# Other widths for four weight groups, and other places for steps in a hand-written order: a change to a two-layer hybrid encoder trunk

## The chip, the core and the metric

The kernel runs on one core of a Trainium2 chip. The metric is the device time of one execution in microseconds (us). Five engines work side by side on a core, each through its own instructions in order: TensorE (PE in the profile, PEld its weight loads), VectorE (DVE), ScalarE (ACT), GpSimd (POOL) and SyncE (SP). Here SP only issues DMAs, and POOL issues DMAs and clears a few tiles.

## The reference

`x` is 256 rows of 2048 columns, `mem` 256 rows of the same width. Two layers follow each other. A layer multiplies `x` by one wide input matrix and cuts the product into eleven parts:

```python
h = x @ w_in
a_q, a_k, a_v, a_z, b_q, b_k, b_v, b_z, b_lr, m_q, m_z = jnp.split(h, cuts, axis=-1)
y_a = chunk_band_attention(a_q, a_k, a_v, rel_table)     # 8 heads of 128
o_b = gla_chunk_recurrence(b_q, b_k, b_v, log_g)         # 4 heads, chunks of 64
y_m = memory_attention(m_q, mk, mv)                      # 4 heads, mk, mv = mem @ w_mem_kv
y = jnp.concatenate([y_a * silu(a_z), y_b * silu(b_z), y_m * silu(m_z)], axis=-1)
x = layer_norm(DEEPNORM_ALPHA * x + y @ w_out, ln_g, ln_b)
```

Group A is softmax attention with a relative bias, group B gated linear attention (GLA) whose gates come from a product of rank 16 (`b_lr`), group M softmax attention into the memory. `y_b` is `o_b` after an RMS norm.

## The kernel before, in words

**Groups and pieces.** Every large product is done in groups. A group is a stripe of weight columns, up to 512 wide, against all 2048 rows of the weight: eight pieces of two k-slices each (`as_group`, L274). For a piece SP loads the fp32 weights into `raw`, ACT writes a rounded copy `wh`, and DVE subtracts to get the rest, `wl` (`piece`, L136, and `parts`, L122). PE then does three products for each k-slice and each of two row blocks: high x with high weight, low x with high weight, high x with low weight (`as_products`, L266). So a piece is twelve matmuls and a group 96. `raw`, `wh` and `wl` have four buffers each, so at most four converted pieces, and four raw ones behind them, can lie ready ahead of PE. The sums of a group stand in a pair of PSUM banks, of which there are two pairs (`psd`).

**Turned data.** Q, K, gates and softmax rows must be transposed for their next use. `turned` (L530) does that without PE: DVE transposes blocks of 32 by 32 into a scratch tile, POOL writes it to a DRAM tile `home`, and four more POOL DMAs read it back in the other order. The reader of the turned tile is either PE itself or a generator that copies it once more (`placed`, L521; `gated`, L509; `gla_turned`, L493; `norm_rows`, L692).

**The order.** PE and SP run in exactly the order in which the program issues instructions. DVE, ACT and POOL are put in order by a planner with its own estimates of times and with priorities; the work of `piece` has a high priority (`AHEAD`). Small work is written as Python generators, and a step of one is let in between two pieces of a group. `tick` (L52) does that: it moves a counter on, by 1 for a piece of 512 columns and by n / 512 for a narrower one (L285). First it runs the entries of `side` whose due time has come. Then it runs one step of one `active` generator that is due. A generator yields the number of ticks until its next step. `waiting` holds generators not yet begun; two may be active while GLA runs, three afterwards. `finish` (L76) ticks until given generators are done, without issuing pieces.

**A layer.** Memory values and keys; in layer 1 also the transposes of the normalised `x`, and `restored`. Then a group for GLA's q and k, then the values: 1552 columns (16 of `b_lr`, 512 of `b_v`, 1024 of `a_v`) in four groups of 388 (`values`, L850). Two of these stand ahead of the loop over `half` at L878, one in each round behind Q and K of four heads. GLA begins with the first round, and its steps lie between the pieces. `finish(laid)` at L883 waits until the turned Q and K of the round have been handed over; then its four heads join `waiting`. The memory queries follow the loop (L888), then the gate groups BZ, AZ0, AZ1 and MZ, each SiLU-ed, turned and multiplied by `gated` or `gla_gate` into the operands `yq` of the output product. The output groups take these operands in quarters: the dictionary `need` says at which piece which `gated` must be done (L908, L959). Each output group adds the residual `res` (L660) and collects statistics; the layer norm follows. In layer 0 `res` is loaded from `xn` by one DMA at L862, after the second value group. The last layer loads `ln_g` and `ln_b` as rows, converts them and writes them into four-row tiles (`norm_rows`); they are read in the last matmuls.

**Due times.** `staged` (L804) puts `placed` on `side` 5 ticks after the group that was turned (L809). `gated` is due 6 ticks after its group (L909). `gla_turned` waits 2 and then 6 ticks (L499). A head of group A (`a_head`) does its scores and softmax, waits 9 ticks for the turned probabilities, does the values' product, and ends 2 ticks later. A memory head (`m_head`) waits 7 (L599), converts, waits 2, multiplies, and ends 2 later.

Of the kernel before, what the change touches and what calls it, by code (L numbers as in the profile page):

```python
# [9 lines left out]
F32R = mybir.dt.float32r  # L10
# [8 lines left out]
P = 128  # L19
# [17 lines left out]
def hybrid_trunk_kernel(  # L37
# [84 lines left out]
    def parts(hi, lo, src):  # L122

        act.copy(hi, src)  # L124
        dve.tensor_tensor(lo, src, hi.bitcast(F32), op=ALU.subtract)  # L125
# [10 lines left out]
    def piece(src, n, kp=2, home=None):  # L136

        with tc.high_priority(AHEAD):
            raw = wp.tile([P, kp, n], F32, name=nm("raw"), tag="raw")
            if home is None:  # L140
                hi, lo = (wp.tile([P, kp, n], F32R, name=nm(w), tag=w) for w in ("wh", "wl"))
            else:
                hi, lo = home
            if isinstance(src, list):
                w = n // len(src)
                for i, part in enumerate(src):
                    sp.dma_start(raw[:, :, i * w:(i + 1) * w], part.rearrange("p (k n) -> p k n", k=kp))
            else:
                sp.dma_start(raw.rearrange("p k n -> p (k n)"), src)
            parts(hi, lo, raw)  # L150
        return hi, lo
# [122 lines left out]
    def as_group(src, xq, n, kp=2, first=None, need={}):  # L274

        acc = psd.tile([P, 2, 512], F32, name=nm("acc"), tag="acc")
        for pc in range(16 // kp):
            if first is not None and pc % 2 == 0:
                xq.append(load_quarter(first[pc // 2]))
            finish(need.get(pc, ()))  # L280
            w = piece(src[pc], n, kp)
            for kk in range(kp):
                for t in range(2):
                    as_products(acc[:, t, :n], t, xq, w, pc * kp + kk, kk)
            tick(n / 512)  # L285
        return acc
# [206 lines left out]
    def gla_turned(yraw, ng, y):  # L493

        yT = []
        for par in range(2):
            yT.append(hd.tile([P, 4, P], F32, name=nm("yT"), tag=("gq", "gk")[par]))
            turned(P, (yT[par], yraw[:, 2 * par:2 * par + 2].rearrange("p t d -> p (t d)")))
            yield 2 + 4 * par  # L499
        for par in range(2):  # L500
            for t in range(2):
                for b in range(2):
                    hi, lo = (x.rearrange("p k (t a j) -> p k t a j", t=2, j=32)[:, b * 2 + par, t] for x in y[:2])
                    src = yT[par].rearrange("p a (t b j) -> p t b a j", t=2, j=32)[:, t, b]
                    act.activation(hi, src, AF.Copy, scale=ng[:, 0:1])
                    dve.scalar_tensor_tensor(lo, src, ng[:, 0:1], hi.bitcast(F32), op0=ALU.mult, op1=ALU.subtract)
            yield 1
# [67 lines left out]
    def m_head(h, q, mk, mv, y, laid):  # L575

        while not all(g in done for g in laid):
            yield 1
        pb = bank()
        for t in range(2):  # L580
            o = pb[:, t * 256:(t + 1) * 256]
            qh, ql = (x[:, h, t * P:(t + 1) * P] for x in q)
            kh, kl = (x[:, h] for x in mk)
            mm(o, qh, kh, True, False)
            mm(o, ql, kh, False, False)
            mm(o, qh, kl, False, True)
        mx = small([P, 2], "mx", 4)
        zs = small([P, 2], "zs", 4)
        dve.tensor_reduce(mx, pb.rearrange("p (t m) -> p t m", t=2), AX.X, ALU.max, negate=True)
        dve.tensor_scalar(mx, mx, SCALE, None, op0=ALU.mult)  # L590
        s = scratch([P, 2, 256])
        for t in range(2):
            act.activation(s[:, t], pb[:, t * 256:(t + 1) * 256], AF.Exp, bias=mx[:, t:t + 1], scale=SCALE, accum_out=zs[:, t:t + 1])
        dve.reciprocal(zs, zs)
        for t in range(2):
            dve.tensor_scalar(s[:, t], s[:, t], zs[:, t:t + 1], None, op0=ALU.mult)
        pT = hd.tile([P, 4, 128], F32, name=nm("pT"), tag="qe" if h % 2 else "gb_")
        turned(128, (pT, s.rearrange("p t m -> p (t m)")))
        yield 7  # L599
        ph, pl = scratch([P, 2, 256], F32R), scratch([P, 2, 256], F32R)  # L600
        for t in range(2):
            parts(*(x.rearrange("p m (t a j) -> p t m a j", t=2, j=32)[:, t] for x in (ph, pl)),
                  pT.rearrange("p a (t m j) -> p t m a j", t=2, j=32)[:, t])
        yield 2
        po = bank()
        for m in range(2):
            vh, vl = (x[:, m, h * P:(h + 1) * P] for x in mv)
            mm(po[:, 0:256], vh, ph[:, m], m == 0, False)
            mm(po[:, 0:256], vl, ph[:, m], False, False)
            mm(po[:, 0:256], vh, pl[:, m], False, m == 1)  # L610
        act.copy(y, po[:, :256])
        yield 2
# [76 lines left out]
            pool.dma_start(raw[i * 16:i * 16 + 16], src[l].rearrange("(k p) -> k p", p=P))  # L689
        return raw, hd.tile([P, 32], F32, name=nm("gbT"), tag="pairs1")  # L690

    def norm_rows(l):  # L692

        rows = []
        for i in range(2):
            cs = slice(i * 1024, (i + 1) * 1024)
            raw, hi, lo, both = (hd.tile([P, 1024], F32R if j else F32, name=nm("gbrow"), tag="qk", bufs=4)
                                 for j in range(4))
            pool.dma_start(raw[0:1], ln_g[l:l + 1, cs])
            pool.dma_start(raw[1:2], ln_b[l:l + 1, cs])  # L700
            parts(hi[:2], lo[:2], raw[:2])
            pool.dma_start(both[0:2], hi[:2])
            pool.dma_start(both[2:4], lo[:2])
            rows.append(both)
        return rows

    def norm_last(accs, rest, stats, gb, rows, more):

# [91 lines left out]
    for l in range(L):  # L800
# [3 lines left out]
        def staged(g, x, raw, place):  # L804
            acc = as_group(halves(g), x, 512)
            raw = raw.rearrange("p (t a) n -> p t a n", t=2) if raw.shape[2] == P else raw.rearrange("p (t a) (b n) -> p t (a b) n", t=2, n=P)
            turned(P, *((raw[:, t], acc[:, t]) for t in range(2)))
            gen = placed(raw, place)
            side.append((gen, now[0] + 5))  # L809
            return [gen]  # L810

        mk = [per.tile([P, 4, T], F32R, name=nm("mk"), tag=f"mk{i}") for i in range(2)]
# [34 lines left out]

        asv = per.tile([P, 2, 1552], F32, name=nm("asv"), tag="asv")

        def values(i):  # L850
            acc = as_group(w388[l, i], xq, 388)
            act.copy(asv[:, :, i * 388:(i + 1) * 388], acc[:, :, :388])

        lr = hd.tile([P, 2, P], F32R, name=nm("lr"), tag="qe")
        pool.memset(lr.bitcast(F32), 0.0)
        values(0)
        for i in (0, 32):
            act.copy(lr[:, :, i:i + 16], asv[:, :, :16])
        dve.tensor_tensor(lr[:, :, 16:32], asv[:, :, :16], lr[:, :, :16].bitcast(F32), op=ALU.subtract)
        values(1)  # L860
        if l == 0:
            sp.dma_start(res, xn.rearrange("(t p) d -> p t d", p=P))  # L862
        bias = {}

        def load_bias(h):
# [9 lines left out]
        gens = [[gla(*gp, gq, gk, lr, asv, yraw[0])]]  # L875
        waiting.extend(gens[0])
        linear[:] = gens[0]
        for half in range(2):  # L878
            q, k = (hd.tile([P, 4, T], F32, name=nm("qk"), tag="qk", bufs=4) for _ in range(2))
            laid = staged(G_AQ0 if half == 0 else G_AQ1, xq, yraw[3], lambda src, at, q=q: act.copy(at(q), src))  # L880
            laid += staged(G_AK0 if half == 0 else G_AK1, xq, k, None)
            values(2 + half)
            finish(laid)  # L883
            kv = k.rearrange("p x y -> p (x y)").rearrange("p (ta g j) -> p g ta j", g=4, j=32)
            gens.append([a_head(half * 4 + h, load_bias, bias, q[:, h], kv[:, h], asv, yraw[1 + half][:, h]) for h in range(4)])
            waiting.extend(gens[-1])
        q = [hd.tile([P, 4, T], F32R, name=nm("mq"), tag="qk", bufs=4) for _ in range(2)]
        laid = staged(G_MQ, xq, yraw[3], lambda src, at: parts(at(q[0]), at(q[1]), src))  # L888
        gens.append([m_head(h, q, mk, mv, yraw[3][:, h], laid) for h in range(4)])
        waiting.extend(gens[-1])  # L890


# [7 lines left out]
        for i, g in ((1, G_AZ0), (2, G_AZ1), (3, G_MZ)):  # L900
            acc = as_group(halves(g), xq, 512)
            yq.append(operand())
            zT = hd.tile([P, 2, 4, P], F32, name=nm("zT"), tag="qk", bufs=4)
            sz = [scratch([P, 512]) for _ in range(2)]
            for t in range(2):
                act.activation(sz[t], acc[:, t], AF.Silu)  # L906
            turned(P, *((zT[:, t], sz[t]) for t in range(2)))
            need[i * 2] = [gated(zT, yraw[i], gens[i], yq[i])]  # L908
            side.extend((x, now[0] + 6) for x in need[i * 2])  # L909
        finish(gens[0])  # L910


# [5 lines left out]
            for dst, src in zip(gb[n], (ln_g, ln_b)):  # L918
                pool.dma_start(dst, src[l:l + 1, columns(n)].to_broadcast([P, 512]))

        rows = norm_rows(l) if last else None
        for n in range(WO_N):
            if last:
                gb.append((scratch([P, 512]), scratch([P, 512])))
# [139 lines left out]
```

## Time and profile before

| | us |
|---|---|
| three runs: lowest, median, highest | 906.75, 909.83, 910.12 |
| the profiled execution | 906.32 |
| its span, first to last instruction | 904.5 |
| granted TensorE clock, mean | 0.998 |
| DMA moved in the span | 211.34 MB, mean 234 GB/s |

The profile is of one execution. Its page gives the busy time of each engine, the span in 40 slices (a digit is the busy share in tenths), the chain of work that ended last, and the costliest groups of instructions. A group line reads: line, engine, operation, output tile `<-` input tiles, shape, count `|` busy us, mean ns of one `|` idle us of the engine just before them, and what ended the idle time. In timelines a row is start us, duration us, engine, line, operation, tiles, shape, count, and in brackets the idle time before it and its releaser. In the chain in order of time a row is start us, us, engine, tile, line and count. In the list of waits a row is: who waited `<-` for whom: us in total, times, longest. A row of stretches has the window, its length, the busy us (and count) of PE, PEld, DVE, ACT and POOL, the granted clock, the DMA share and GB/s. Matmuls are pipelined and their ends are modelled, so starts are safer than durations. L102 is the one line that issues all matmuls, L124 and L125 are the two operations of `parts`, so tiles tell the groups apart: `acc` is a group's PSUM tile, `bk` a single bank for small work, `wh` and `wl` the converted weights.

### The profile page before, as it was taken

The page shows a single profiled execution, that of the slowest core. Times are in us where ns is not written, and L with a number is a line of the kernel's source. Part 1 is how long each engine was busy: PE and PEld are TensorE (multiplying, and loading weights), DVE is VectorE, ACT ScalarE, POOL GpSimd, SP SyncE. Part 2 cuts the span into 40 slices and gives each one's busy share as a digit, 9 for nine tenths or more (in the row PEclk, how much of TensorE's full clock was granted, in tenths as well). Part 3 has the DMA queues.
Part 4 walks back from the last instruction along what each step waited for, and adds up shares of the span by engine and source line. Part 5 has one row for each costly group of instructions (what it writes and reads, how often), then busy time and mean ns, then how long its engine had stood idle before and what let it go on. Part 6 is the DMA issues. An engine that isn't in the chain of part 4 may idle for free.

```text
span 904.5 us, 13856 instructions
## 1 busy us (share of the span) xinstructions
PE 897.8 (99%) x4798; PEld 768.2 (85%) x4798; DVE 607.2 (67%) x878; ACT 477.2 (53%) x687; POOL 197.8 (22%) x369
## 2 busy tenths in 40 slices
PE   9999999999999999999999999999999999999997
PEld 8889988988988888888888898898898888888885
DVE  6765478766566676565587676777756586666766
ACT  6654465574545566433476445655744465655440
POOL 0002012116243553200000220221071434334000
PEclk9999999999999999999999999999999999999999
DMA  9977976858977998776675687658698879888652
GB/s 308 324 210 212 310 234 183 262 167 259 273 230 224 265 275 264 232 254 192 210 247 192 201 250 224 203 186 249 189 267 242 261 218 276 253 260 274 211 164 93
DMA packets 145974, 211.34 MB, mean 234 GB/s; under 512 B 15464, under 2 KB 117224, under 8 KB 145648
## 3 DMA queue, kind: packets, MB, share of 16 engines
q1 hardware_dynamic: 130544, 173.28, 61.5%
q0 software_dynamic: 15072, 36.79, 14.3%
q8 instruction: 37, 0.61, 0.3%
q10 hardware_dynamic: 288, 0.39, 0.1%
q14 instruction: 33, 0.27, 0.1%
HBM read 192.02 MB, written 18.35 MB: 233 GB/s over the span
## 4 chain that ended last, share of the span: by engine, by line
PE 99%; DMA 0%; DVE 0%; ACT 0%; issue 0%
PE acc L102 90%; PE bk L102 8%; PE bk L630 0%; DMA raw<-w 0%; PE bk L399 0%; ACT res L786 0%; DVE stats L771 0%; PE bk L346 0%; DVE res L770 0%; ACT wh L124 0%; DVE res L722 0%; DVE mvt L725 0%; PE bk L774 0%; ACT nparts L124 0%; DVE rs_u L733 0%
## 5 line engine op out<-in xcount | busy, mean ns | idle before, releaser
L102 PE MATMUL acc<-wh,x 128*128 128x512 f32 (+2 forms) x2452 | 736.9, 382 | 0.2 <-ACT wh L124 0.2
L102 PEld LDWEIGHTS acc<-wh,x 128*128 128x128 f32 x2452 | 453.7, 188 | 73.5 <-ACT wh L124 0.5
L125 DVE TENSOR_TENSOR wl<-raw,wh 128x1024 fp32r<-128x1024 f32 (+3 forms) x321 | 368.1, 1152 | 196.9 <-ACT wh L124 194.3
L124 ACT CAST wh<-raw 128x1024 fp32r<-128x1024 f32 (+3 forms) x321 | 318.7, 996 | 327.9 <-PE acc L102 250.4
L102 PE MATMUL acc<-wl,x 128*128 128x512 f32 (+2 forms) x1226 | 465.0, 380 | 0.0
L102 PEld LDWEIGHTS acc<-wl,x 128*128 128x128 f32 x1226 | 230.4, 188 | 39.1 <-DVE wl L125 0.4
L537 POOL DMA_DIRECT2D home<-sc x66 | 36.9, 560 | 455.0 <-DVE sc L535 447.0
L540 POOL DMA_DIRECT2D pT<-home x96 | 52.7, 555 | 46.4 <-DMA home<-sc 19.3
L540 POOL DMA_DIRECT2D qk<-home x56 | 30.5, 551 | 13.3 <-DMA home<-sc 7.9
L540 POOL DMA_DIRECT2D zT<-home x48 | 26.2, 553 | 29.9 <-DMA home<-sc 19.3
L540 POOL DMA_DIRECT2D yr<-home x48 | 26.1, 551 | 20.2 <-DMA home<-sc 14.8
L535 DVE STREAM_TRANSPOSE sc<-sc 128x512 f32<-128x512 f32 (+1 forms) x36 | 22.7, 643 | 2.0 <-ACT sc L906 1.4
L560 ACT ACTIVATE sc<-sc,mx 128x128 f32<-128x128 f32 (+1 forms) x32 | 14.4, 450 | 16.3 <-DVE mx L558 16.2
L535 DVE STREAM_TRANSPOSE sc<-acc 128x512 f32<-128x512 f32 x26 | 17.0, 692 | 6.9 <-PE acc L102 6.9
L518 DVE TENSOR_TENSOR sc<-zT,yr 128x256 f32<-128x256 f32 x24 | 8.9, 417 | 13.8 <-DMA zT<-home 13.8
L124 ACT CAST x<-sc 128x512 fp32r<-128x512 f32 x20 | 11.8, 616 | 4.4 <-DVE sc L518 3.1
L125 DVE TENSOR_TENSOR x<-sc,x 128x512 fp32r<-128x512 f32 x20 | 13.2, 686 | 0.7 <-ACT x L124 0.7
L125 DVE TENSOR_TENSOR x<-raw,x 128x1024 fp32r<-128x1024 f32 x5 | 6.1, 1212 | 11.3 <-ACT x L124 11.3
L102 PEld LDWEIGHTS bk<-pT,asv 128*128 128x128 f32 x64 | 12.0, 189 | 1.8
L391 DVE TENSOR_TENSOR sc<-gk,sc 128x512 f32<-128x512 f32 x12 | 8.3, 691 | 7.2 <-ACT sc L389 7.2
L102 PE MATMUL bk<-qk,qk 128*128 128x128 f32 (+1 forms) x64 | 13.1, 326 | 0.0
L102 PE MATMUL bk<-pT,asv 128*128 128x256 f32 (+1 forms) x64 | 13.0, 326 | 0.0
(209 smaller groups left out, 557.0 us busy)
## 6 DMA issues: line engine op xcount, KB each, us to landing
raw<-w SPq DMA_DIRECT2D x387, 256.0 KB, 4.4
raw<-w SPq DMA_DIRECT2D x62, 512.0 KB, 5.1
raw<-w SPq DMA_DIRECT2D x64, 388.0 KB, 3.9
home<-sc POOLq DMA_DIRECT2D x50, 256.0 KB, 4.8
qk<-home POOLq DMA_DIRECT2D x56, 64.0 KB, 5.7
bias<-relw SPq DMA_DIRECT2D x16, 192.0 KB, 5.2
yr<-home POOLq DMA_DIRECT2D x48, 64.0 KB, 4.2
home<-sc POOLq DMA_DIRECT2D x16, 192.0 KB, 3.2
```

The costliest lines, as they stand in the source:

```text
L102: pe.matmul(o, l, r, start=start, stop=stop, skip_group_check=True)
L124: act.copy(hi, src)
L125: dve.tensor_tensor(lo, src, hi.bitcast(F32), op=ALU.subtract)
L391: dve.tensor_tensor(kl, gkf, dd, op=ALU.mult)
L518: dve.tensor_tensor(o, z, r, op=ALU.mult)
L535: dve.transpose(blocks.rearrange("p b (g j) -> p g b j", j=32), src.rearrange("p (g b j) -> p g b j", b=4, j=32))
L537: pool.dma_start(homes[-1], blocks)
L540: pool.dma_start(dst[b * 32:(b + 1) * 32], home[:, b].rearrange("(a i) n -> i a n", a=4))
L560: act.activation(s[:, own[t]], s[:, own[t]], AF.Exp, bias=mx[:, t:t + 1], accum_out=zs[:, t:t + 1])
```

## The change

Four things are done together.

- The value groups are 512, 264, 264 and 512 columns wide. The arrays in memory keep their four blocks of 388, so a 512-column group takes its pieces from two blocks (388 + 124 columns) by two DMAs, and a 264-column group from one. The first two groups end at column 776 as before. The other two both stand in the first round of the loop.
- The residual of layer 0 is loaded in four parts of 512 columns, one behind each of the groups Q0, K0, Q1 and K1.
- The heads of the first round join `waiting` behind both value groups; those of the second behind the memory queries, which move into the round in place of the last value group.
- Readers of turned data are handed over later: `placed` 8 ticks after its group if it copies, else 6; `gated` 8; the second step of `gla_turned` 8; `m_head` 8. `norm_rows` becomes a generator on `side`, due 8 ticks after it is put there, with 4 ticks between a load and its conversion.

```diff
 def piece
-                w = n // len(src)
-                for i, part in enumerate(src):
-                    sp.dma_start(raw[:, :, i * w:(i + 1) * w], part.rearrange("p (k n) -> p k n", k=kp))
+                at = 0
+                for part in src:
+                    if len(part.shape) == 2:
+                        part = part.rearrange("p (k n) -> p k n", k=kp)
+                    sp.dma_start(raw[:, :, at:at + part.shape[2]], part)
+                    at += part.shape[2]
 def gla_turned
-            yield 2 + 4 * par
+            yield 2 + 6 * par
 def m_head
-        yield 7
+        yield 8
-    def norm_rows(l):
-        rows = []
+    def norm_rows(l, rows):
         for i in range(2):
             ...
             pool.dma_start(raw[0:1], ln_g[l:l + 1, cs])
             pool.dma_start(raw[1:2], ln_b[l:l + 1, cs])
+            yield 4
             parts(hi[:2], lo[:2], raw[:2])
             pool.dma_start(both[0:2], hi[:2])
             pool.dma_start(both[2:4], lo[:2])
             rows.append(both)
-        return rows
 def staged
-            side.append((gen, now[0] + 5))
+            side.append((gen, now[0] + (6 if place is None else 8)))
-        def values(i):
-            acc = as_group(w388[l, i], xq, 388)
-            act.copy(asv[:, :, i * 388:(i + 1) * 388], acc[:, :, :388])
+        def values(c0, n):
+            src = [[w388[l, j, pc].rearrange("p (k n) -> p k n", k=2)[:, :, max(c0 - j * 388, 0):min(c0 + n - j * 388, 388)]
+                    for j in range(c0 // 388, (c0 + n - 1) // 388 + 1)] for pc in range(8)]
+            acc = as_group(src, xq, n)
+            act.copy(asv[:, :, c0:c0 + n], acc[:, :, :n])
-        values(0)
+        values(0, 512)
-        values(1)
-        if l == 0:
-            sp.dma_start(res, xn.rearrange("(t p) d -> p t d", p=P))
+        values(512, 264)
+        def load_res(i):
+            if l == 0:
+                sp.dma_start(res[:, :, columns(i)], xn.rearrange("(t p) d -> p t d", p=P)[:, :, columns(i)])
+        def staged_queries():
+            q = []
+            def place(src, at):
+                if not q:
+                    q.extend(hd.tile([P, 4, T], F32R, name=nm("mq"), tag="qk", bufs=4) for _ in range(2))
+                parts(at(q[0]), at(q[1]), src)
+            return q, staged(G_MQ, xq, yraw[3], place)
         for half in range(2):
             q, k = (hd.tile([P, 4, T], F32, name=nm("qk"), tag="qk", bufs=4) for _ in range(2))
             laid = staged(G_AQ0 if half == 0 else G_AQ1, xq, yraw[3], lambda src, at, q=q: act.copy(at(q), src))
+            load_res(half * 2)
             laid += staged(G_AK0 if half == 0 else G_AK1, xq, k, None)
-            values(2 + half)
+            load_res(half * 2 + 1)
+            if half == 0:
+                values(776, 264)
+                values(1040, 512)
+            else:
+                mq = staged_queries()
             finish(laid)
             ...
-        q = [hd.tile([P, 4, T], F32R, name=nm("mq"), tag="qk", bufs=4) for _ in range(2)]
-        laid = staged(G_MQ, xq, yraw[3], lambda src, at: parts(at(q[0]), at(q[1]), src))
-        gens.append([m_head(h, q, mk, mv, yraw[3][:, h], laid) for h in range(4)])
+        gens.append([m_head(h, mq[0], mk, mv, yraw[3][:, h], mq[1]) for h in range(4)])
 the gate groups
-            side.extend((x, now[0] + 6) for x in need[i * 2])
+            side.extend((x, now[0] + 8) for x in need[i * 2])
 the last layer
-        rows = norm_rows(l) if last else None
+        rows = []
+        if last:
+            side.append((norm_rows(l, rows), now[0] + 8))
```

## The prediction

> **What bounds the kernel now.** I read the totals and the 40 slices first, then the chain of work that ended last, in total and in order of time.
>
> ```profile
> span 904.5 us, 13856 instructions
> PE 897.8 (99%) x4798; PEld 768.2 (85%) x4798; DVE 607.2 (67%) x878; ACT 477.2 (53%) x687; POOL 197.8 (22%) x369
> PE   9999999999999999999999999999999999999997
> PE 99%; DMA 0%; DVE 0%; ACT 0%; issue 0%
> ```
>
> TensorE is busy in every slice but the last, and it is 99% of the chain. A busy PE need not be PE at its peak, since ends are modelled, so I took starts. Two pieces of the chain in time order hold nothing but full-width products:
>
> ```profile
> 350.53 122.44 PE acc L102 x540
> ...
> 796.26 87.13 PE acc L102 x384
> ```
>
> 122.44 / 540 = 0.2267 us and 87.13 / 384 = 0.2269 us for one 512-column matmul: the same pace in a stage rich in other work and in a bare one, so nothing holds PE up there. Where a head's step comes in between, the chain shows this:
>
> ```profile
> 280.49 0.66 PE bk L102 x4
> 281.15 2.77 PE acc L102 x12
> ```
>
> Twelve matmuls take 2.77 us behind a step and 12 x 0.2267 = 2.72 us without one: a step costs its own matmuls plus 0.05 us, and never a wait. The only real stalls that I found between the start-up and the end are two of layer 1, seen in PE's timeline as a first product with `wl` that lasts 0.43 us:
>
> ```profile
> 596.03 0.43 PE L102 MATMUL acc<-wl,x 128*128 128x512 f32 x1
> ...
> 613.17 0.43 PE L102 MATMUL acc<-wl,x 128*128 128x388 f32 x1
> ```
>
> The usual 512-column row is 0.39 and the usual 388-column one 0.34: 0.04 + 0.09 = 0.13 us in all. So the change can save PE's own pace, 0.13 us of stalls, and little else; what it can lose is the cover by which converted weights run ahead of PE.
>
> **The change part by part.** *Value groups.* PE's timeline has the pace by width, first and last row of a run (three matmuls to a row of this kind and its partner):
>
> ```profile
> 94.67 0.34 PE L102 MATMUL acc<-wl,x 128*128 128x388 f32 x1
> ...
> 105.80 0.34 PE L102 MATMUL acc<-wl,x 128*128 128x388 f32 x1
> ```
>
> ```profile
> 891.67 0.28 PE L102 MATMUL bk<-wl,x 128*128 128x256 f32 x1
> ...
> 894.19 0.28 PE L102 MATMUL bk<-wl,x 128*128 128x256 f32 x1
> ```
>
> The first two are 21 such rows apart: (105.80 - 94.67) / 63 = 176.7 ns at 388 columns. The others are 7 apart: 2.52 / 21 = 120.0 ns at 256. No row has 264; between 120.0 and 176.7 a straight line puts it at 120.0 + 8 x 56.7 / 132 = 123.4 ns. I take that, since 256 is nearest; the ends are 120.0 and 176.7. A group has 96 matmuls (16 slices of k, two row blocks, three products). Per layer before: 384 x 176.7 = 67.85 us. After: 192 x 226.7 + 192 x 123.4 = 67.22 us. Gain 0.63 us a layer, **1.26 us** in both. With 120.0 it would be 2.6 us, with 176.7 a loss of 19.2 us. 388 is simply a bad width: the line from 256 to 512 (120.0 to 226.7) would have it at 175.0 ns.
>
> The Trainium skill ("TensorE: Matmul & The Clock Gate", section "Back-to-back issue gap") gives an isolated gap of N / 2.4 + 2.5 ns. That is a straight line in N, by which four groups of 1552 columns in all cost the same however they are cut: 164.2 x 4 = 656.7 = 2 x 215.8 + 2 x 112.5, a gain of nothing. The trace doesn't lie on it (120.0, 176.7 and 226.7 against 109.2, 164.2 and 215.8).
>
> Converting the weights costs ACT one cast and DVE one subtraction a piece:
>
> ```profile
> L125 DVE TENSOR_TENSOR wl<-raw,wh 128x1024 fp32r<-128x1024 f32 x248 | 301.4, 1220 | 153.2 <-ACT wh L124 151.0 <-DMA raw<-w 1.5
> L125 DVE TENSOR_TENSOR wl<-raw,wh 128x776 fp32r<-128x776 f32 x64 | 61.2, 964 | 41.7 <-ACT wh L124 41.5
> L125 DVE TENSOR_TENSOR wl<-raw,wh 128x512 fp32r<-128x512 f32 x7 | 4.8, 693 | 2.0 <-ACT wh L124 1.8
> L124 ACT CAST wh<-raw 128x1024 fp32r<-128x1024 f32 x248 | 260.1, 1051 | 254.8 <-PE acc L102 189.4 <-DMA raw<-w 30.0 <-issue 16.1
> L124 ACT CAST wh<-raw 128x776 fp32r<-128x776 f32 x64 | 53.6, 842 | 69.2 <-PE acc L102 61.0 <-DMA raw<-w 4.4 <-issue 3.3
> ```
>
> A 264-column piece has 528 elements: about 0.71 us on DVE and 0.64 on ACT from these rows. Old 32 x (0.96 + 0.84) = 57.8 us a layer, new 16 x 2.27 + 16 x 1.35 = 57.9: no change. The issue on SP goes from 32 to 48 DMAs a layer (a 512-column group needs two a piece); pieces of other groups have two each already. Cost 0, hidden by the pieces that wait ready: ACT sat idle behind PE for 61.0 of its 69.2 us before 388-column casts. The cover itself shrinks, though: four converted pieces last PE 4 x 12 x 0.2267 = 10.9 us at 512 columns, 8.5 us at 388, and 5.9 us at 264. That is the one real risk (rival 1).
>
> The 512-column groups fetch 124 of their columns as runs of 496 bytes. The Trainium skill ("DMA: Bandwidth & Descriptors", section "Specifications") puts the line rate at 512 B and more, with a read-modify-write below. By it those loads land later, which the 10.9 us cover would hide, so the sum stays; the trace's weight packets are all longer, and it can't show it.
>
> *Residual in four parts.* Now one DMA of layer 0:
>
> ```profile
> res<-xn SPq DMA_DIRECT2D x1, 2048.0 KB, 9.3
> ...
> 90.00:110.00 20.00, 20.00 (x111) 19.28 (x110) 9.62 (x10) 9.81 (x13) 0.00 (x0) 1.00 0.90 309
> ```
>
> It fills the DMA engines to 0.90 in that window, yet PE is busy for 20.00 of 20.00 us. The parts are 512 KB each, among weights on SP's queue in order, behind Q0, K0, Q1 and K1; they wait for nothing that is not long done, and their reader is the last stage. Gain 0, cost 0 (three more issues).
>
> *Readers handed over later.* Readers of turned data wait in engine order today:
>
> ```profile
> ACT qk L880 <- DMA yr<-home: 8.2, 4, 4.8
> DVE sc L518 <- DMA zT<-home: 13.8, 3, 6.2
> ```
>
> The 4.8 us of ACT is the one that nearly starved PE. The timelines of ACT and DVE show it:
>
> ```profile
> 588.67 0.62 ACT L880 COPY qk<-yr 128x512 f32<-128x512 f32 x1 [4.82 <-DMA yr<-home]
> ```
>
> ```profile
> 584.76 1.22 DVE L125 TENSOR_TENSOR wl<-raw,wh 128x1024 fp32r<-128x1024 f32 x1
> ...
> 594.70 1.21 DVE L125 TENSOR_TENSOR wl<-raw,wh 128x1024 fp32r<-128x1024 f32 x1
> ```
>
> Behind ACT's wait stood the casts, and 9.9 us passed between two conversions; of 10.9 us cover PE missed only 0.04 us (at 596.03). A tick is one 512-column piece, 2.72 us; three ticks later is 8.2 us, more than the 4.8. The wait goes; what is late next is PE itself. Gain 0.04 to 0.13 us; I take **0.1 us**.
>
> *Heads let in later.* A group counts 8 ticks at 512 columns, 6.1 at 388, 4.1 at 264; from the start of the first query group, by the code's yields, heads 0-3 come in at 28.1 (22.1 before), heads 4-7 at 52.1 (44.1). GLA ends at 28.1, so three heads enter at once. Each step issues the same matmuls, transposes and DMAs, at another place. Cost on PE: the same number of steps at 0.05 us; a few may share a gap or part, 0.3 us either way. The last memory head ends at 92.1 (82.1 before), and the last `gated` at 93.1 (90.1), while its product is due at 96.1 in both. The lead falls from 6 ticks (16.3 us) to 3 (8.2 us). The chain that must fit, in the two layers:
>
> ```profile
> 377.91 0.76 DVE L518 TENSOR_TENSOR sc<-zT,yr 128x256 f32<-128x256 f32 x2 [6.18 <-DMA zT<-home]
> ...
> 382.67 1.29 DVE L125 TENSOR_TENSOR x<-sc,x 128x512 fp32r<-128x512 f32 x2
> ```
>
> ```profile
> 822.82 0.76 DVE L518 TENSOR_TENSOR sc<-zT,yr 128x256 f32<-128x256 f32 x2
> ...
> 825.54 1.20 DVE L125 TENSOR_TENSOR gbrow<-gbrow,gbrow 2x1024 fp32r<-2x1024 f32 x1
> ...
> 830.98 1.29 DVE L125 TENSOR_TENSOR x<-sc,x 128x512 fp32r<-128x512 f32 x2
> ```
>
> That is 6.0 and 9.4 us; the second has the `gbrow` conversion inside it, which the change puts later. So it fits. `norm_rows` itself is cut in two and starts 8 ticks later; its rows are read only in the last 20 us. Cost 0.
>
> On POOL head 7 and two memory heads (65.1 to 67.1) come to stand right ahead of `zT` of the next gate (68.1, read at 76.1).
>
> ```profile
> L540 POOL DMA_DIRECT2D pT<-home x96 | 52.7, 555 | 46.4 <-DMA home<-sc 19.3
> ...
> home<-sc POOLq DMA_DIRECT2D x50, 256.0 KB, 4.8
> ```
>
> A turned tile takes five issues of 0.555 and 4.8 us of landing between: three times 7.6, and 10.4 for the two halves of `zT`, 33 us or 12 ticks from 65.1. DVE may then wait a tick or two at `zT`, 3 to 5 us inside a cover of 10.9. Cost 0, with rival 4 as its other end.
>
> **Sum:** -1.26 - 0.1 = -1.4 us. The profiled execution took 906.3 us (span 904.5 and 1.8 around it), the median of the three runs is 909.83, so the span by itself would come to about 903.1 and the median to **908.4**.
>
> **Rivals.** (1) *Converted weights run out in a 264-column group.* The second such group meets GLA's longest burst. DVE in layer 1:
>
> ```profile
> 605.69 0.96 DVE L125 TENSOR_TENSOR wl<-raw,wh 128x776 fp32r<-128x776 f32 x1
> ...
> 612.13 4.13 DVE L125 TENSOR_TENSOR wl<-raw,wh 128x776 fp32r<-128x776 f32 x4
> ```
>
> 6.4 us without a conversion used up the 8.5 us of the 388-column cover (the stall at 613.17). With 5.9 us of cover the same order loses 2.6 us more: it decides from 5.9 - (8.5 - 6.4) = 3.8 us without a conversion on. One layer: 909.8 - 1.4 + 2.6 = 911.0; both 913.6. Against it: the order on DVE and ACT is laid anew, and the copies that waited for DMAs are out of it. (2) *The cut gives nothing*: at 126.7 ns for 264 columns, (4 x 176.7 - 2 x 226.7) / 2, the gain is gone, and the 0.1 leaves 909.7. For it speaks only that 264 is unmeasured. This is where the Trainium skill's line ("TensorE: Matmul & The Clock Gate", section "Back-to-back issue gap") comes out. (3) *Weight loads bind*: PEld is at 85%, and if a 264-column matmul can't beat 176.7 ns the time is 909.8 + 19.2 = 929.0. The 120.0 rows speak against it. (4) *The shorter lead is missed*: 9.4 us against 8.2, up to a late `zT` (6.2 more): +1.2 to +7, 909.7 to 915.4. (5) *The margins matter more than the profile shows*: two of the three runs took 3 us longer than the fastest; if those were starved pieces, the change ends all, 906.75 - 1.4 = 905.3.
>
> **How the numbers follow.** Forecast 0.50, (1) 0.24, (2) 0.08, (3) 0.03, (4) 0.05, (5) 0.10. Range: from case 5 less the 0.65 us that half the way to 120.0 would add (384 x 1.7 ns), 904.7, to case 1 in both layers, 913.6. A measurement of this kernel tells 0.5% (4.5 us) from no change: faster needs under 905.3 (half of case 5 and the forecast's lower edge, 0.08), slower over 914.4 (case 3, and the ends of 1 and 4, 0.08), within it 0.84.
>
> **What would show it.** Right: 264-column products 123 ns apart; no product with `wl` longer than its fellows between 550 and 620 us; ACT's wait for `yr` gone; PE still 99%. Wrong: PE waiting for `wl` in the second 264-column group; 264-column starts over 127 ns apart; PE waiting for `x` at the third quarter of the first output groups.

## The result, and the profile after

| | before | changed |
|---|---|---|
| median of six runs | 909.98 us | 919.48 us |
| lowest to highest | 906.75 to 911.05 | 916.26 to 921.61 |
| the profiled execution, its span | 906.32, 904.5 | 919.13, 917.4 |

The ratio is 1.0116, with a 95% interval of 1.0097 to 1.0135: slower by 1.2%, where 908.4 (904.7 to 913.6) was forecast. The ratios in this document are estimates of their own with an interval, and not quotients of the two medians (here 1.0104); differences of 0.1 to 0.2% shouldn't be read from either.

The changed kernel's page: the span, PE's busy time, and the slices of PE and of its granted clock.

```profile
span 917.4 us, 13946 instructions
PE 901.8 (98%) x4798; PEld 753.7 (82%) x4798; DVE 606.7 (66%) x878; ACT 480.5 (52%) x691; POOL 198.0 (22%) x369
PE   9999999989999999999999999999899999999997
PEclk9999999999999999999999999999899999999999
PE 94%; ACT 2%; DMA 2%; DVE 2%; issue 0%; SPq 0%; DVEq 0%; ACTq 0%
```

PE has the same 4798 matmuls, and dips in one slice of each layer (about 200 and 650 us). PE has fallen from 99% to 94% of the chain. Its bare pace is untouched: the chain in time order has, in the output groups of layer 1,

```profile
836.49 59.93 PE acc L102 x264
```

59.93 / 264 = 0.227 us. So the time went at a few places. The list of waits, for PE alone, names them:

```profile
PE acc L102 <- ACT wh L124: 5.8, 3, 2.9
PE acc L102 <- DVE wl L125: 2.3, 3, 0.9
```

PE's timeline has both kinds in layer 0, and the first also in layer 1:

```profile
164.44 0.39 PE L102 MATMUL acc<-wl,x 128*128 128x264 f32 x1 [0.92 <-DVE wl L125]
```

```profile
205.77 0.73 PE L102 MATMUL acc<-wh,x 128*128 128x512 f32 x2 [2.92 <-ACT wh L124]
207.03 0.80 PE L102 MATMUL acc<-wl,x 128*128 128x512 f32 x1 [0.52 <-DVE wl L125]
```

```profile
657.39 1.22 PE L102 MATMUL acc<-wh,x 128*128 128x512 f32 x2 [2.47 <-ACT wh L124]
```

The stop at 164 us is rival 1, in the second 264-column group; layer 1 has its like at 616 us, of 0.91 us. The stop at 203 to 207 us was in no rival. Stretches around it (us, then busy us of PE, PEld, DVE, ACT and POOL, the clock, the DMA share and GB/s):

```profile
190.00:200.00 10.00, 10.00 (x48) 8.38 (x47) 4.57 (x11) 6.66 (x17) 0.00 (x0) 1.00 0.04 9
200.00:206.00 6.00, 3.08 (x15) 2.30 (x14) 2.60 (x8) 2.64 (x8) 0.58 (x1) 1.00 0.85 258
206.00:210.00 4.00, 3.48 (x9) 2.48 (x9) 3.96 (x8) 3.04 (x7) 0.50 (x1) 0.57 1.00 315
...
658.00:664.00 6.00, 5.96 (x15) 4.21 (x14) 5.96 (x11) 3.31 (x6) 2.73 (x5) 0.50 0.96 325
```

Read from the right: from 190 to 200 us, shortly before the stop, the DMA engines stand at 0.04, though weights are needed. PE lives on what was converted before, then stops, and when it comes back its clock is halved for some time. Why no load was issued stands in SP's timeline and in SP's own list of waits:

```profile
176.36 0.46 SPq L874 DMA_DIRECT2D bias<-relw  x1
176.92 0.94 SPq L149 DMA_DIRECT2D raw<-w  x2
177.91 0.47 SPq L874 DMA_DIRECT2D bias<-relw  x1
178.66 1.26 SPq L149 DMA_DIRECT2D raw<-w  x2
198.66 0.34 SPq L874 DMA_DIRECT2D bias<-relw  x1
199.10 4.39 SPq L149 DMA_DIRECT2D raw<-w  x8
```

```profile
SPq L874 <- DVE mx L561: 38.2, 2, 19.2
```

L874 is `load_bias`. Three heads enter on neighbouring ticks, and each begins by loading the bias for the head after next. The third load needs the tile of head 0 (there are four), and head 0 has only just entered: its bias is read by L556 on DVE, behind GLA's last steps. DVE's timeline has that reader, and the next operation, by which the list names the wait:

```profile
198.07 0.56 DVE L556 SCALAR_TENSOR_TENSOR sc<-bk,bias 128x384 f32<-128x384 f32 x1
198.67 0.61 DVE L561 TENSOR_REDUCE mx<-sc 128x1 f32<-128x128 f32 x2
```

SP issues in order, so all weights stood 19 us behind one load of 192 KB. The price, from the rows: 2.92 + 0.52 us idle and 4.0 x 0.43 = 1.7 us of lost clock in layer 0; 2.47 us and 6.0 x 0.50 = 3.0 us in layer 1. That is 10.6 us; the two stops in 264-column groups add 1.8, and the narrow pace takes 2.4 off. (10.0 of the 12.9 us between the two spans; the rest is in small stops and switches that I did not sort.)

### The profile page after: what moved, and what is told of

Read it like the earlier page. It is cut to its first block, busy times and chain, and to the rows that moved or that the text cites. A ratio compares the mean times of both kernels' runs of the same rounds, so it can differ in the third digit from the quotient of the medians.

```text
span 917.4 us, 13946 instructions
## 1 busy us (share of the span) xinstructions
PE 901.8 (98%) x4798; PEld 753.7 (82%) x4798; DVE 606.7 (66%) x878; ACT 480.5 (52%) x691; POOL 198.0 (22%) x369
## 4 chain that ended last, share of the span: by engine, by line
PE 94%; ACT 2%; DMA 2%; DVE 2%; issue 0%; SPq 0%; DVEq 0%; ACTq 0%
PE acc L102 86%; PE bk L102 7%; DMA raw<-w 2%; ACT sc L479 1%; ACT wh L124 1%; PE bk L633 0%; ACT yr L474 0%; DVE wl L125 0%; DVE yr L485 0%; ACT L295 0%; ACT asv L856 0%; DVE yr L477 0%; DVE sc L556 0%; DVE sc L395 0%; PE bk L402 0%
## 5 line engine op out<-in xcount | busy, mean ns | idle before, releaser
L102 PEld LDWEIGHTS acc<-wh,x 128*128 128x128 f32 x2452 | 449.2, 189 | 90.5 <-ACT wh L124 7.3
L556 DVE SCALAR_TENSOR_TENSOR sc<-bk,bias 128x384 f32<-128x384 f32 x16 | 8.6, 538 | 9.9 <-PE bk L102 7.9
L124 ACT CAST x<-raw 128x1024 fp32r<-128x1024 f32 x5 | 5.3, 1051 | 15.7 <-DMA raw<-memT 13.1
```

What stands on the lines that cost most here:

```text
L102: pe.matmul(o, l, r, start=start, stop=stop, skip_group_check=True)
L556: dve.scalar_tensor_tensor(s, pb[:, :384], SCALE, bias[h], op0=ALU.mult, op1=ALU.add)
```

## The experiments

Each ratio is to the kernel before, measured on the same chip in the same session; its medians in the three sessions were 908.42, 909.24 and 908.55 us.

**The bias loads moved out of the way.** All else of the change stays.

```diff
 def a_head
-        if h + 2 < 8:
-            load_bias(h + 2)
         ...
         yield 9
+        if h + 4 < 8:
+            load_bias(h + 4)
-        load_bias(0)
-        load_bias(1)
+        for h in range(4):
+            load_bias(h)
```

> The changed kernel, with four bias tiles loaded ahead and each next one loaded only after its head's wait of 9 ticks, so that no bias load on SP's queue waits for a buffer when three heads enter at once. Theory A (the load of the fifth bias tile waits on SP for head 0, 19 us in each layer, and holds all weight loads behind it; PE then idles some 3.5 us and runs 6 us at half clock): the idle time at 203 to 207 us and 651 to 658 us goes, about 5.5 us a layer, and the time falls from 919.5 to about 908.5, SP's wait for the bias gone. Rival B (ACT is late at GLA's end, with the squares, an eviction of 1.0 us and two table loads of 1.28 us, and starves PE by itself): PE still stops at the same place; at most 2 us are won, 917.5. Rival C (three heads at once overload DVE): 917 or more.

908.98 us, ratio 1.0007 (0.9992 to 1.0022). The same two stretches and PE's waits in its profile:

```profile
190.00:200.00 10.00, 10.00 (x48) 8.37 (x47) 6.03 (x13) 8.05 (x19) 0.00 (x0) 1.00 0.52 151
200.00:206.00 6.00, 6.00 (x30) 4.96 (x29) 4.58 (x11) 4.10 (x10) 0.58 (x1) 1.00 0.56 179
```

```profile
PE acc L102 <- DVE wl L125: 0.9, 1, 0.9
```

The DMA engines work through the stretch and PE never stops in it: theory A. SP's list of waits has no bias load any more. GLA's end and three heads at once are still there, so B and C fall. Within the intervals, the whole loss of 1.2% was this one wait; of the stops for weights only the one at 164 us is left.

**The same wait put into the kernel before.** One edit, no part of the change: `tag="bias", bufs=4` becomes `bufs=3`.

> The kernel before with three bias tiles in place of four, and nothing else: the load for the head after next must now wait on SP for the head just let in wherever two heads come in on neighbouring ticks (heads 1 and 2, heads 4 and 5). Theory A (a bias load that waits on SP holds the weights behind it and empties PE): 3 to 6 us are lost at each such place, of which each layer has two, so 915 to 930, with SP's wait at the bias load tens of us long, though no part of the change is in it. Rival B or C (the loss belongs to GLA's end or to the heads' bunching): no stall, 908 to 910.

934.41 us, ratio 1.0282 (1.0262 to 1.0302), above the range. SP's waits and PE's first stop:

```profile
SPq L867 <- DVE sc L553: 46.0, 4, 20.8
SPq L867 <- DVE mx L558: 31.5, 2, 15.7
```

```profile
203.73 1.22 PE L102 MATMUL acc<-wh,x 128*128 128x512 f32 x2 [4.70 <-ACT wh L124]
```

So the mechanism needs nothing but a bias load that comes too soon after the head whose tile it takes.

**The widths taken back**: `values` at 388 columns four times in the changed kernel.

> The changed kernel with the four value groups at 388 columns again; all else of the change stays. Theory A: the stall in the first of the two groups of the round goes (cover 8.5 us), the one behind SP's bias wait stays, PE's pace costs 0.6 us a layer: 919.5 - 2.4 + 1.2 = 918.3. Rival E (the cut, with its split loads, is what makes the change slow): back to 910.

916.21 us, 1.0086 (1.0061 to 1.0111). SP's wait at the bias load is still there (32.0 us in all), and so is most of the loss: the widths are not its main cause. In this profile PE's waits for `wl` are 1.0 us in all against 2.3.

**The widths alone**, each group in its old place in the kernel before.

> The kernel before with the value groups of 512, 264, 264 and 512 columns alone, each in its old place in the order; residual, heads and readers as before. Theory A: PE's pace wins 1.2 us, heads still come in one by one, so SP's bias wait doesn't bind; the third group, of 264 columns, meets GLA's burst and stalls 0 to 1.2 us a layer: 908.8 to 911.2. Rival E: 917 or more.

910.83 us, 1.0028 (1.0014 to 1.0043): a little slower. PE's timeline right behind the first 264-column group:

```profile
108.44 0.72 PE L102 MATMUL acc<-wh,x 128*128 128x512 f32 x2 [3.02 <-ACT wh L124]
109.70 0.50 PE L102 MATMUL acc<-wl,x 128*128 128x512 f32 x1 [0.54 <-DVE wl L125]
```

```profile
105.00:110.00 5.00, 1.44 (x7) 0.80 (x6) 1.31 (x2) 2.69 (x3) 0.00 (x0) 1.00 1.04 337
110.00:115.00 5.00, 5.00 (x17) 3.92 (x16) 3.27 (x4) 3.14 (x3) 0.00 (x0) 0.66 0.76 226
```

DMA is at its full share: the residual's 2 MB come in just then, and the four pieces ahead of PE are short ones.

**The residual in four parts, with the widths and alone.** The first is the kernel before with the change's `values` and `load_res`, the second with `load_res` only.

> The kernel before with the four widths and the residual in four parts; heads and readers as before. If the one load of 2 MB is what starves PE at 105 to 110 us in the cut alone (3.0 us without weights, and half clock behind it, 5.3 us in all), because 264-column pieces give less cover ahead of it, this is 4 to 5 us under the cut alone, 905.5 to 907. If the stall there belongs to the width and its split loads alone, it stays at 910 to 911.

> The kernel before with the residual in four parts alone. In its profile PE never waits around the load of 2 MB, so the theory that only starved pieces cost time gives no change, 908 to 909. If its slower runs are runs in which the margin of 0.9 us at 106 us was missed, the median falls towards the fastest runs, 906.5 to 907.5.

906.72 us, 0.9979 (0.9965 to 0.9992), and 908.23 us, 1.0000 (0.9983 to 1.0018). The parts are worth nothing at 388 columns and 0.5% (1.0028 against 0.9979) with the narrow group in front of Q0. In the profile of widths and parts the stop of 3.02 us is gone; all that PE waits for `wh` is this:

```profile
PE acc L102 <- ACT wh L124: 0.6, 2, 0.4
```

Widths and parts together have the lowest median and ratio of the study, 0.2% under the kernel before; two versions further down lie too close to them to be told apart. The second reading offered for the parts alone, that the median falls towards the fastest runs, was not borne out.

**Where the narrow group stands.** Two runs: 388 and 388 columns in the rounds with 512 and 264 in front; and the first experiment's kernel with 512 ahead of 264 in the round.

```diff
-            values(*((776, 264), (1040, 512))[half])
+            values(*((776, 388), (1164, 388))[half])
```

```diff
-                values(776, 264)
-                values(1040, 512)
+                values(776, 512)
+                values(1288, 264)
```

> The kernel before with 512 and 264 columns for the first two value groups, 388 and 388 for the two in the rounds, and the residual in four parts. If the 264-column group costs only where it meets GLA's burst, this is the best of all: PE's pace wins 0.6 us and no cover is lost, 906.5 to 907.5, and below the four widths by what these lose in the third group, about 1 us. If not, the same as with the four widths.

> As the run before it, and the two value groups of the first round in the other order, 512 and then 264 columns, so that GLA's longest burst on DVE meets pieces of 2.72 us. Theory A (the stall of 1.07 us at 163 and 615 us is the short cover of four 264-column pieces, 5.9 us): it goes, 1.2 us a layer, and the time is 2.4 us below that of the run before, about 906, some 4 us under the kernel before. Rival D (the stall belongs to the burst's order on ACT and DVE, whatever the width): it stays within 0.3 us, 908.5. A third outcome would be that GLA's last steps now meet the 264-column group and stall there.

907.68 us, 0.9998 (0.9984 to 1.0012), just above the range and no better than the four widths; its interval and theirs overlap, so this tells nothing. The swap gave 913.42 us, 1.0056 (1.0037 to 1.0074), worse by 0.5% than without it, against both theories' times. Its profile is of the slowest of its eight runs (916.09 us). The third outcome isn't in it: the 264-column group of layer 0 begins at 179.73 us, and PE stops ahead of it, in the 512-column group:

```profile
169.04 0.73 PE L102 MATMUL acc<-wh,x 128*128 128x512 f32 x2 [1.00 <-ACT wh L124]
170.57 0.50 PE L102 MATMUL acc<-wl,x 128*128 128x512 f32 x1 [0.80 <-DVE wl L125]
```

There DVE starts no conversion from 157.13 to 169.30 us, 12.2 us where the cover of four 512-column pieces is 10.9; 3.89 us of that it is idle before a step of GLA that waits for a DMA. So in layer 0 the burst's order stops PE in spite of the wide pieces, as rival D had it. Layer 1 has no such stop, with the swap or without it. A new stop came up, where PE's product of a head waits for turned probabilities:

```profile
PE bk L102 <- DMA pT<-home: 6.0, 2, 4.4
PE acc L102 <- ACT wh L124: 1.6, 3, 1.0
PE acc L102 <- DVE wl L125: 1.2, 2, 0.8
```

The third head's five POOL DMAs queue behind those of two other heads and, by the timeline, behind the two stores of Q1's turned tile. So the 9 ticks of a head may be too short when three go at once; that was not tried by itself.

**Later readers and later heads.** Three runs in the kernel before, all with `norm_rows` left as it was: the readers alone; widths, parts and readers; the same with 388 and 388 in the rounds. And the changed kernel with the bias loads moved and 388 and 388 in the first round.

> The kernel before with the later readers alone. By the theory that PE's rare waits for the memory queries go: 0.3 to 1.5 us under the kernel before. If the later readers cost, above it.

> The change without its later heads: four widths, residual in four parts, readers handed over later, but heads come in behind the third value group of the round as before, and the memory queries follow the loop. If the later readers only take waits away (ACT and DVE at turned data, and the memory queries that now and then hold PE's first product of a memory head for 1 to 3 us), this is at or under the cut with the residual alone: 905 to 906.7. If handing over later costs (readers that come too late), 908 or more.

> As the run before it, with 388 and 388 columns for the two value groups in the rounds. Without the stall of 0.9 us in the 264-column group, and with 0.3 us a layer less of PE's pace: 0.3 to 0.6 us better than the run before it in layer 0, about 905.5. If the short cover doesn't matter any more once the readers are late, 0.6 us worse.

> The changed kernel with the bias tiles loaded ahead and 388 columns for the two value groups of the first round: both stalls found so far are gone, the later heads stay. If nothing else in the later heads costs, 906 to 907.5; if their bunching costs by itself, 908.5 or more.

908.44 us, 1.0000 (0.9984 to 1.0016); 907.29 us, 0.9981 (0.9964 to 0.9998); 907.11 us, 0.9984 (0.9969 to 0.9999); 908.24 us, 0.9999 (0.9981 to 1.0017). The first three miss what was hoped for, and the fourth lies between its two readings. In the fourth's profile the stop in the first round's narrow group has shrunk from 0.91 to 0.39 us at 388 columns, but PE still waits 1.2 us for `wl` in all, so not both stalls are gone. Later readers neither win nor lose. Without later heads the versions lie 0.2% under the kernel before, with them level with it (1.0007 and 0.9999). These intervals overlap, and the versions differ in the bias loads and `norm_rows` too, so that later heads cost 0.2% by themselves is possible, not shown.

## Why the prediction was wrong

**The step that failed** is "Heads let in later", in its sentence "Each step issues the same matmuls, transposes and DMAs, at another place. Cost on PE: the same number of steps at 0.05 us". It followed the bunched heads' DMAs on POOL, and not the one that a head issues on SP. By its own ticks it had the answer: head 0 used to come in at 22.1, and head 2 only behind GLA's end at 28.1; now "three heads enter at once". On PE the scores of heads 0 and 2 of layer 0 start at 174.16 and 198.07 us before, and at 195.21 and 202.03 after. SP runs up to eight pieces ahead of PE (four raw and four converted), and the row that gives the wait away stands in the old kernel's list of SP's waits, on which the prediction doesn't draw:

```profile
SPq L867 <- DVE sc L553: 17.6, 3, 8.5
```

8.5 us were already spent there, hidden by pieces that lay ready. Priced at nothing, it cost 1.1% (1.0116 against 1.0007).

**Value groups.** Right in sign, and undersized: in the changed kernel 264-column rows start at 160.02 and, eight rows on, at 162.91, 2.89 / 24 = 120.4 ns where 123.4 was taken. PE's pace gives 1.2 us a layer, not 0.63. Rival 2, which needed 126.7 ns, is out. The short runs, of which the prediction could show nothing, landed in 3.7 us (124 KB) where the 388 KB beside them took 4.3; these rows show no price of theirs.

**Rival 1** was right in mechanism and place, the second 264-column group, and too dear: 0.92 us where 2.6 a layer was the price. The estimate took 2.1 us (8.5 less 6.4) off the cover, as if they were lost ahead of any burst. In the changed kernel none was lost. DVE's conversions around the burst of layer 0:

```profile
156.22 0.71 DVE L125 TENSOR_TENSOR wl<-raw,wh 128x528 fp32r<-128x528 f32 x1 [0.73 <-ACT wh L124]
...
163.69 3.59 DVE L125 TENSOR_TENSOR wl<-raw,wh 128x528 fp32r<-128x528 f32 x4
```

These are 7.5 us, more than the old 6.4. But PE first had the rest of GLA's 96 products, to 157.12 us, and then four whole pieces, 48 products or 5.9 us, to 163.03.

**Residual.** "Gain 0, cost 0" holds at the old widths. With the narrow group it is the part that pays, for the same reason as rival 1, short cover; the prediction looked for that only where GLA bursts.

**Later readers.** Their 0.1 us is below what runs can tell (1.0000), but the step to it was wrong as well: "The wait goes", and it didn't. In the changed kernel ACT's waits for `yr` are more than before (8.2 us, longest 4.8):

```profile
ACT qk L897 <- DMA yr<-home: 11.1, 6, 2.9
```

With the readers alone they are 8.4 us, the longest 5.6 at 591.61 us, and PE stops for weights behind it, 0.82 us at 598.90. Why a later handover doesn't take the wait away stays open. What did go is PE's wait for the memory queries, 1.0 to 2.1 us in three profiles with the old readers; it shows in no run with the later ones.

**Rivals 3, 4 and 5**: weight loads did not bind at 176.7 ns; in the changed kernel PE never waited for `yq`, and at most 0.6 us for a memory head's probabilities. The spread of runs did not shrink in the changed kernel (5.4 us over six runs, 4.3 before). With widths and parts and no later heads three versions span 3.6 to 3.9 us where the kernel before spans 7.1 and 7.4, but over a third of the runs, so rival 5 stays open there.

**The clock** was left out of every price. The stops of 2.9 and 2.5 us cost another 1.7 and 3.0 us at reduced speed.

## What to carry to other kernels

When a step is moved, list every DMA that it issues, on every queue, with the buffer that each one waits for and the distance to the last reader of that buffer; a load that is harmless on its own holds everything behind it on an in-order queue. A kernel with a bound engine at 99% can still lose a per cent: look at the queue waits that are hidden now, and ask how many pieces hide them. Cover is counted in time, not in buffers: four buffers of narrower pieces are less of it.

## What the runs showed of the hardware

PE's granted clock fell to half after idle gaps of 2.47 us (657 us; 0.50 until 664) and 2.92 us (206 us; 0.57 over 4 us), and not after the gap of 0.92 us at 164 us. With four groups of 388 columns 1.87 us, with another 0.53 us soon after, were enough (0.50 from 206 to 208 us); in the swap 1.00 and 0.80 us at 169 to 171 us were not (1.00). Read by single microseconds, the half clock lasted 3.4 us in layer 0 of the changed kernel (206.6 to 210.0) and 6.8 us in layer 1 (657.1 to 664.0). The Trainium skill ("TensorE: Matmul & The Clock Gate", section "HAM oscillation — how this bites in real kernels") asks that idle gaps stay under about 3.4 us; here shorter ones were enough.

264 columns went at 120.4 ns and 256 at 120.0, where a line through 256, 388 and 512 columns has 3 ns between them. Whether something other than columns sets the pace there wasn't tried.
